# A hybrid decoder layer: start addresses of the matmul operands brought to one residue modulo 256 bytes

## The chip, the cores and the metric

The kernel runs on 1 core of a Trainium2 chip. The metric is the device time of one execution in microseconds (us). Before the change the median of 3 runs is 2601.95 us (2596.57 to 2602.49).

## What is computed

One decoder layer on 2048 tokens of width 1024, all in float32. Cut to what matters here:

```python
mod = silu(c) @ w_ada + b_ada                    # six vectors: sh_m, sc_m, gt_m, sh_f, sc_f, gt_f
h = rmsnorm(x, g_mix) * (1 + sc_m) + sh_m
q, k, v, f_logit, u = split(h @ w_in)            # 8 heads x 64; u: 32 groups x 16
log_f = log_sigmoid(f_logit + b_fgate)
attn = rmsnorm(forgetting_attention(q, k, v, log_f), g_attn_out)   # causal softmax(qk/8 + cum_i - cum_j) v
ssm = rmsnorm(s5_ssm(u, ...), g_ssm_out)         # scan, GELU z, z * sigmoid(z @ w_glu + b_glu)
x = x + gt_m * (concat(attn, ssm) @ w_out)
h = rmsnorm(x, g_ffn) * (1 + sc_f) + sh_f
gate, val = split(h @ w_up)                      # 2 x 2816
x = x + gt_f * ((silu(causal_dwconv(gate)) * val) @ w_down)
out = rmsnorm(x, g_final)
```

## The kernel before, in words

**Arithmetic.** Every large product is done in three matmuls in the fp32r format: each float32 operand is split into a rounded part (`hi`) and a remainder (`lo`), and hi·hi, hi·lo and lo·hi are summed in PSUM. Such a matmul has a stationary operand (`lhsT`, 128x128, the weights, which PE loads by a separate LDWEIGHTS) and a moving operand (`rhs`, mostly 128x512, that is 2048 bytes in each partition). The page names a matmul as out<-moving,stationary, so `up_x<-hh,w_hi` moves `hh` past weights from `w_hi`. While one matmul streams its moving operand, PE already loads the weights of the next.

**Stages.** The 2048 tokens are four blocks of 512. From 0 to about 650 us the kernel computes the modulation vectors (`ada_first`), the projections (`proj_u` with `token_rows`, L437, and `proj_qkv`, L470), the SSM's tables (`ssm_tables`) and the SSM (`ssm`), with the first attention block. From about 650 to 1820 us attention of blocks 1 to 3 (`att_max` L952; `att_main` L997, L998, a 128-wide mask matmul L1000, L1018, L1022) is woven by the scheduler between the output projection (L1232) and the feed-forward of blocks 0 and 1 (`up` L1258, `down` L1290 to L1292). From about 1960 to 2340 us `up_pair` computes the up-projection of blocks 2 and 3 together, with a two-by-two scheme of seven products (L1382, banks `up_x`, `up_y`, `up_z`). The rest is their down-projection (`down_both`, L1530 to L1532 and L1612, banks `acc_x` to `acc_z`).

**Weights.** `Weights.raw` brings a slice of the weights from HBM into one of two `w_raw` buffers of `WSLOT` = 1056 columns (L78); `split` makes `w_hi` on ScalarE (L86) and `w_lo` on VectorE (L87). All slices have at most 1024 columns but two: the weights of the columns 1536 to 1799 in `proj_u` have 4 x 264 = 1056. These go through `load` into `wu_hi` and `wu_lo` tiles of their own. A scheduler with a timeline model orders the instructions of all engines, so any edit can move others.

**Where tiles start.** Tiles lie in SBUF in pools. Pools on the left are stacked upward from a low address: `const`, `w`, `small`, `h`, the stages' own. Pools with `side="right"` are stacked downward from the top: `vq`, `att`, `late`, `ring`. A tile's start address is the sum of what lies below (or above) it, in steps of 32 bytes. A 128x512 float32 tile has 2048 bytes, so tiles of one pool keep one residue modulo 256 where all its tiles are multiples of 256 bytes, and slices of 128 columns (512 bytes) keep it too. In the built program the start addresses modulo 256 are:

| tiles of the 512-wide matmuls | pool side | before | after |
|---|---|---|---|
| `w_hi`, `w_lo` (weights) | left | 64 | 224 |
| `h_hi`, `h_lo`, `act_hi`, `act_lo`, `yt0` to `yt7`, `kx0`, 35 of 53 `ring`, 18 of 52 `hh` | left | 64 | 224 |
| `qb`, `kb`, `qa`, `ka`, `ph`, `pl`, `vv`, 28 `hh` | right | 160 | 224 |
| 18 `ring`, 4 `hh` | right | 224 | 224 |
| 2 `hh` (one in each of two longer `vq` buffers) | right | 160 and 192 | 224 and 0 |
| `w_raw` (raw weights) | left | 64 and 192 | 224 |

Modulo 512 the left tiles stand at 320 before and 480 after; the right tiles of the third row at 416 before and 224 after; the `ring` and `hh` of the fourth row at 480 both times. `wu_hi` and `wu_lo`, which are moving operands of 256 or 264 columns, start at 0 and 128 before and at 32 and 160 after, with the stationary `h_hi` and `h_lo` at 64 and 224.

Of the kernel before, what the change touches and what calls it, by code (L numbers as in the profile page):

```python
# [12 lines left out]
F32 = mybir.dt.float32  # L13
# [4 lines left out]
ALU = mybir.AluOpType  # L18
# [4 lines left out]
P = 128  # L23
# [4 lines left out]
TB = S // NB  # L28
H = 8
NG = 32  # L30
# [2 lines left out]
NFF = DFF // P  # L33
EPS = 1e-6
NEG = -1e30
WSLOT = 1056
RSQRT_MAGIC = float(0x5F3759DF)
MAGIC = 12582912.0
FFG = (6, 6, 5, 5)
# [27 lines left out]
class Weights:  # L67
# [6 lines left out]
    def raw(self, off, n, raw=None):  # L74
        if raw is None:
            raw = self.pool.tile([P, WSLOT], F32, name="w_raw", tag="w_raw", bufs=2)
        src = self.flat[off : off + P * n].rearrange("(p n) -> p n", p=P)
# [18 lines left out]
        return hi, lo  # L96

    def load(self, off, n, hi, lo):
        self.split(self.raw(off, n), n, hi, lo)

    def get(self, off, n):
        return self.split(self.raw(off, n), n)
# [18 lines left out]
def hybrid_layer(ctx, tc, x, c_t, w_ada, b_col, gains, w_flat, bf_row, a_re, a_im, log_dt,  # L121
                 sb_re, sb_im, sc_re, sc_im, dskip, glu, bglu, conv, out):
    nc = tc.nc
    V, A, G, T, Q = nc.vector, nc.scalar, nc.gpsimd, nc.tensor, nc.sync

    const = ctx.enter_context(tc.tile_pool(name="const", bufs=1))
    wpool = ctx.enter_context(tc.tile_pool(name="w", bufs=2))
    small = ctx.enter_context(tc.tile_pool(name="small", bufs=4))
    dram = ctx.enter_context(tc.tile_pool(name="scratch", bufs=1, space=DRAM))
    mark = [None]  # L130

    @contextmanager
    def behind(ins=None):
# [78 lines left out]
    off = 0  # L212
# [9 lines left out]
    for g in FFG:  # L222
        gs = []
# [5 lines left out]
    def opened(stack, name, **kw):  # L229
        return stack.enter_context(tc.tile_pool(name=name, reuse_waits="tile", **kw))  # L230
# [3 lines left out]
    vq = opened(vq_ctx, "vq", bufs=2, side="right")  # L234
# [27 lines left out]
    def max_ps():  # L262
        return am_ps()
# [3 lines left out]
    def am_ps():  # L267
        n = next(am_n) % 4 if sc_extra else 0
        if n >= 2:
            return sc_extra[n - 2]()  # L270
        return att_ps.tile([P, 512], F32, name="sc_ps", tag="sc", bufs=2)

    def vq_a(name, shape, dtype):
        return vq.tile(shape, dtype, name=name, tag="vq_a")
# [359 lines left out]
        V.tensor_tensor(out=cn, in0=cn, in1=n, op=ALU.subtract)  # L634

    r8 = const.tile([P, NPAIR], F32, name="r8")
    hb = const.tile([P, NG], F32, name="hb")

    def cmul(eng, ore, oim, ar, ai, br, bi, t):

# [7 lines left out]
    def ssm_tables(pp):  # L648
        misc_ps = prep_ps
        sh = [P, NPAIR]  # L650
        def tl(nm, shape=sh, **kw):
            return pp.tile(shape, F32, name=f"tb_{nm}", tag=f"tb_{nm}", **kw)
# [1 line left out]
        Q.dma_start(ar, a_re)  # L654
        Q.dma_start(ai, a_im)
        Q.dma_start(ld, log_dt)
        Q.dma_start(hb, bglu)
        V.tensor_scalar(out=hb, in0=hb, scalar1=0.5, scalar2=None, op0=ALU.mult)
        br, bi = tl("br", [P, NPAIR, 16]), tl("bi", [P, NPAIR, 16])
        cr, ci = tl("cr", [P, NPAIR, 16]), tl("ci", [P, NPAIR, 16])  # L660
        Q.dma_start(br, sb_re)
# [73 lines left out]
        for i0, tr_, ti_ in ((3, pl_re, pl_im), (7, ph_re, ph_im)):  # L735
            G.memset(tr_[:, :, 0:1], 1.0)
            G.memset(ti_[:, :, 0:1], 0.0)
            for i in range(4):
                m = 1 << i
# [69 lines left out]

    def ssm(sp, sps):  # L810

        fts = [sp.tile([P, 2, 2, P], F32, name=f"ft{i}", bufs=1) for i in range(2)]
        for ft in fts:
            G.memset(ft, 0.0)
# [90 lines left out]
        for p in range(NPAIR + 1):  # L905
            nxt = None
            if p < NPAIR:
                if p % 4 == 0:
                    vin = []
                    for kb in range(2):  # L910
                        t = sp.tile([P, 8, P], F32, name="vin", tag=f"vin{kb}")
                        src = u_d[kb * 1024 : (kb + 1) * 1024, (p // 4) * P : (p // 4 + 1) * P]
# [17 lines left out]
    def att_max(b, h):  # L930
# [16 lines left out]
        def part(ch, s):  # L947
            if s == 0:
                load(ch)
            n = max(256, (s + 1) * P) if ch == b else 512  # L950
            ps = max_ps()
            T.matmul(ps[:, 0:n], lhsT=qa[0:66, s * P : (s + 1) * P], rhs=ka[ch][0:66, 0:n], start=True, stop=True)  # L952
            to = mx[:, s, ch : ch + 1]
            if ch == b:
                sc = ps[:, 0 : (s + 1) * P]
                V.tensor_tensor_reduce(out=sc, in0=sc, in1=mask_q[:, (3 - s) * P :], scale=1.0, scalar=3.0 * NEG,
                                       op0=ALU.add, op1=ALU.max, accum_out=to)
            else:
                V.reduce_max(out=to, in_=ps[:, 0:n], axis=AX.X)
# [19 lines left out]
    def att_main(b, h, qa, qb, ka):  # L979
# [4 lines left out]
        def part(ch, i):  # L984
# [9 lines left out]
            cs = slice(c0, 512)  # L994
            ks = slice(i * P, (i + 1) * P)
            ps = am_ps()
            T.matmul(ps[:, cs], lhsT=kbt[:, ks], rhs=qb[:, cs], start=True, stop=False)  # L997
            T.matmul(ps[:, cs], lhsT=ka[ch][:, ks], rhs=qa[:, cs], start=False, stop=(ch != b))  # L998
# [120 lines left out]
    with tc.tile_pool(name="prep", bufs=1) as pp, tc.tile_pool(name="wu", bufs=1) as wup:  # L1119
        rows0 = load_x(2)  # L1120
        wu = load_u_weights(wup, vfu_slots[4:6])
        ada_first()
        batches = ssm_tables(pp)
        wu += load_u_weights(wup, vfu_slots[6:8])
        marks = []
        for b in (2, 3, 1):
            h = proj_u(b, rows0 if b == 2 else load_x(b), wu)
            marks.append(mark[0])
        batches(marks + marks[-1:])
        rows0 = load_x(0)  # L1130
        proj_qkv(1, h, pair_ps(qs_psum))
        ada_late(4, "gf")
        h = proj_u(0, rows0, wu)
        ada_late(3, "sf")
        forget()
        ada_cols()
        fold_gain(mod["gf"], 8)
        ada_late(2, "tm")
# [317 lines left out]
    def down_both(ap, rp, dps, misc):  # L1456
# [8 lines left out]
        def w_cols(f0, n, d):  # L1465
            raw = wpool.tile([P, WSLOT], F32, name="w_raw", tag="w_raw", bufs=2)
            o, c0 = 0, 0
            for g, m in enumerate(FFG):
                lo, hi = max(f0, c0), min(f0 + n, c0 + m)
                if lo < hi:  # L1470
                    so, sn = dn_slots[g][d]
                    view = w_flat[so : so + P * sn].rearrange("(p n) -> p n", p=P)
                    k = (hi - lo) * P
                    weights.last = Q.dma_start(raw[:, o : o + k], view[:, (lo - c0) * P : (hi - c0) * P])
                    o += k
                c0 += m
            return raw
# [231 lines left out]
    with tc.tile_pool(name="ssm", bufs=2) as sp, tc.tile_pool(name="ssm_ps", bufs=1, space=PSUM) as sps:  # L1709
        with tc.high_priority():  # L1710
            ssm(sp, sps)
# [215 lines left out]
```

## Time and profile before

| | |
|---|---|
| median of 3 runs | 2601.95 us |
| the profiled execution: time, span | 2602.08 us, 2600.4 us |
| mean granted TensorE clock of that execution | 0.98 |
| PE busy | 2506.6 us, 12107 matmuls |
| DVE busy | 2046.1 us |
| ACT busy | 1253.3 us |

A matmul's record in the trace is longer than the distance to the next one's start, since matmuls are pipelined: records overlap. Where PE never waits, the distance between starts is what a matmul costs. A row of a timeline gives start, length, engine, line, operation, out<-moving,stationary and shapes; rows of one line that follow each other with the same tiles are merged (x2). In the view of one line a row gives the shortest, median and longest record in ns. "PEclk" is the granted clock.

### The profile page before, as it was taken

How to read it: one execution, taken by the hardware profiler on the slowest of the kernel's cores; microseconds unless marked ns; L12 is line 12 of the kernel's file. 1: busy time of each engine (PE TensorE's matmuls, PEld its weight loads, DVE VectorE, ACT ScalarE, POOL GpSimd, SP SyncE). 2: the span in 40 equal slices, each digit the busy share in tenths (PEclk: the TensorE clock that was granted, in tenths of full speed). 3: DMA queues.
4: the chain of work that ended last, by engine and by line, in shares of the span. 5: the costliest groups of instructions: out<-in, count | busy, mean ns of one | idle time of the engine just before them, and what ended most of it. 6: DMA issues, size and time to landing. Idle time of an engine off the chain costs nothing.

```text
span 2600.4 us, 35785 instructions
## 1 busy us (share of the span) xinstructions
PE 2506.6 (96%) x12107; PEld 2046.8 (79%) x12107; DVE 2046.1 (79%) x3952; ACT 1253.3 (48%) x2120; POOL 152.2 (6%) x160
## 2 busy tenths in 40 slices
PE   5999899998999999999999999999989999999997
PEld 3888778887788888888878888888767888887876
DVE  7989688976787878787877777776589888886777
ACT  3423255643464545465655555556554554553213
POOL 0001000000000000000000000000002333320000
PEclk8899999998899999999999999999999999999998
DMA  8577987667456655656557555556733443448573
GB/s 300 171 240 228 287 275 212 205 195 239 165 195 219 197 191 185 196 170 217 189 192 231 183 172 191 177 177 222 242 105 126 173 155 133 158 144 294 195 272 124
DMA packets 269319, 516.36 MB, mean 199 GB/s; under 512 B 27952, under 2 KB 114864, under 8 KB 269136
## 3 DMA queue, kind: packets, MB, share of 16 engines
q1 hardware_dynamic: 267312, 508.84, 59.3%
q0 software_dynamic: 1280, 4.20, 0.4%
q8 instruction: 96, 1.57, 0.3%
q10 hardware_dynamic: 544, 1.05, 0.1%
q14 instruction: 87, 0.71, 0.1%
HBM read 374.32 MB, written 139.59 MB: 198 GB/s over the span
## 4 chain that ended last, share of the span: by engine, by line
PE 81%; DVE 8%; DMA 6%; ACT 2%; issue 2%; SPq 1%; POOL 0%; POOLq 0%; DVEq 0%; ACTq 0%
PE ff_ps L1258 18%; PE ff_ps L1232 7%; PE up_x L1382 7%; PE up_z L1382 4%; PE up_y L1382 4%; PE ff_ps L1290 3%; PE ff_ps L1292 3%; PE ff_ps L1291 3%; PE o_ps L1018 2%; PE o_ps L1022 2%; PE acc_x L1612 2%; PE vq_ps L470 2%; PE qs_ps L470 2%; DMA wada<-in_w_ada 2%; PE proj_ps L437 2%
## 5 line engine op out<-in xcount | busy, mean ns | idle before, releaser
L86 ACT CAST w_hi<-w_raw 128x1024 fp32r<-128x1024 f32 (+4 forms) x187 | 173.2, 927 | 268.6 <-DMA w_raw<-in_w_flat 69.7
L1258 PE MATMUL ff_ps<-h_hi,w_lo 128*128 128x512 f32 x704 | 277.7, 394 | 1.0 <-DMA w_lo<-wlo 1.0
L1258 PE MATMUL ff_ps<-h_hi,w_hi 128*128 128x512 f32 x704 | 277.7, 396 | 0.6 <-ACT h_hi L388 0.4
L1258 PE MATMUL ff_ps<-h_lo,w_hi 128*128 128x512 f32 x704 | 278.1, 395 | 0.0
L87 DVE TENSOR_TENSOR w_lo<-w_raw,w_hi 128x1024 fp32r<-128x1024 f32 (+4 forms) x187 | 199.7, 1068 | 62.4 <-ACT w_hi L86 51.6
L1009 DVE TENSOR_TENSOR pl<-pf,ph 128x512 fp32r<-128x512 f32 (+1 forms) x320 | 194.7, 618 | 19.8 <-ACT ph L1008 18.9
L1008 ACT CAST ph<-pf 128x512 fp32r<-128x512 f32 (+1 forms) x320 | 177.9, 568 | 61.0 <-PE o_ps L1018 57.2
L1017 DVE TENSOR_TENSOR acc<-acc,pf 128x512 f32<-128x512 f32 (+2 forms) x264 | 159.4, 605 | 44.7 <-ACT pf L1007 39.4
L1007 ACT ACTIVATE pf<-sc_ps 128x512 f32<-128x512 f32 (+3 forms) x184 | 96.3, 528 | 128.3 <-PE sc_ps L998 76.1
L1258 PEld LDWEIGHTS ff_ps<-h_hi,w_lo 128*128 128x128 f32 x704 | 133.0, 189 | 29.9 <-DMA w_lo<-wlo 1.4
L1258 PEld LDWEIGHTS ff_ps<-h_hi,w_hi 128*128 128x128 f32 x704 | 132.9, 189 | 29.4 <-DVE h_f L400 0.7
L1258 PEld LDWEIGHTS ff_ps<-h_lo,w_hi 128*128 128x128 f32 x704 | 132.9, 189 | 28.5 <-issue 0.2
L116 ACT CAST w_hi<-w_raw 128x1024 fp32r<-128x1024 f32 (+2 forms) x100 | 96.5, 965 | 110.6 <-PE ff_ps L1258 50.8
L1291 PE MATMUL ff_ps<-act_lo,w_hi 128*128 128x512 f32 x352 | 138.4, 394 | 0.0
L1292 PE MATMUL ff_ps<-act_hi,w_lo 128*128 128x512 f32 x352 | 138.4, 394 | 0.0
L1290 PE MATMUL ff_ps<-act_hi,w_hi 128*128 128x512 f32 x352 | 138.1, 395 | 0.0
L1018 PE MATMUL o_ps<-ph,vv 128*128 128x512 f32 (+1 forms) x320 | 121.0, 379 | 1.2 <-ACT ph L1008 1.2
L1022 PE MATMUL o_ps<-pl,vv 128*128 128x512 f32 (+2 forms) x312 | 117.0, 377 | 2.5 <-DVE pl L1009 2.3
L1382 PE MATMUL up_x<-hh,w_hi 128*128 128x512 f32 x352 | 112.0, 398 | 3.4 <-ACT hh L385 1.9
L1382 PE MATMUL up_z<-hh,w_hi 128*128 128x512 f32 x308 | 97.6, 398 | 2.9 <-ACT w_hi L86 2.9
L86 ACT CAST w_hi<-s 128x1024 fp32r<-128x1024 f32 (+2 forms) x66 | 62.1, 944 | 78.1 <-DVE s L1583 22.1
L437 PE MATMUL proj_ps<-wu_hi,h_hi 128*128 128x264 f32 (+1 forms) x256 | 76.2, 304 | 13.4 <-ACT h_hi L388 11.7
(673 smaller groups left out, 6863.2 us busy)
## 6 DMA issues: line engine op xcount, KB each, us to landing
w_raw<-in_w_flat SPq DMA_DIRECT2D x193, 512.0 KB
w_lo<-wlo SPq DMA_DIRECT2D x68, 512.0 KB
wlo<-w_lo SPq DMA_DIRECT2D x52, 512.0 KB
kb<-kb SPq DMA_DIRECT2D x80, 256.0 KB
vv<-v SPq DMA_DIRECT2D x80, 256.0 KB
w_raw<-in_w_flat SPq DMA_DIRECT2D x40, 384.0 KB
w_raw<-in_w_flat SPq DMA_DIRECT2D x40, 320.0 KB
wada<-in_w_ada SPq DMA_DIRECT2D x48, 256.0 KB
```

The costliest lines, as they stand in the source:

```text
L86: nc.scalar.copy(hi[:, :n], raw[:, :n])
L87: nc.vector.tensor_tensor(out=lo[:, :n], in0=raw[:, :n], in1=hi[:, :n].bitcast(F32), op=ALU.subtract)
L1008: A.copy(ph[:, cs], pf[:, cs])
L1009: V.tensor_tensor(out=pl[:, cs], in0=pf[:, cs], in1=ph[:, cs].bitcast(F32), op=ALU.subtract)
L1018: T.matmul(o_ps[:, cs], lhsT=vt[:, i, :], rhs=ph[:, cs], start=first, stop=False)
L1022: T.matmul(o_ps[:, cs], lhsT=vt[:, i, :], rhs=pl[:, cs], start=False, stop=(b > 0 and ch == b - 1 and i == 3))
L1232: mark[0] = T.matmul(ps, lhsT=lt, rhs=rt, start=(i == 0), stop=(i == 23))
L1258: T.matmul(ps, lhsT=lt, rhs=rt, start=(n == 0), stop=(n == 23))
L1290: T.matmul(ps, lhsT=a, rhs=ah[:, ts], start=(c == 0), stop=False)
L1291: T.matmul(ps, lhsT=a, rhs=al[:, ts], start=False, stop=False)
L1292: mark[0] = T.matmul(ps, lhsT=bb, rhs=ah[:, ts], start=False, stop=(c == n - 1))
L1382: mark[0] = T.matmul(ps, lhsT=lt, rhs=rt, start=(first and n == 0), stop=(n == 11), skip_group_check=not first)
```

## The change

It has four parts. `WSLOT` becomes 1024, so that a `w_raw` buffer has 4096 bytes instead of 4224; slices of 1056 columns are loaded by `load` in two halves of 528, each with a load, a cast and a subtraction of its own. Two pads are put in: 32 bytes in `const`, 192 bytes in `vq`, behind a first tile of `vq_a`'s size that fixes the order of `vq`'s parts (the third call, of 0 bytes, makes no tile). The GLU bias `hb` (128 bytes) moves from `const` to the SSM's own pool, and its load and its multiplication by 0.5 move with it from `ssm_tables` to the head of `ssm`.

```diff
-WSLOT = 1056
+WSLOT = 1024
...
     def load(self, off, n, hi, lo):
-        self.split(self.raw(off, n), n, hi, lo)
+        m = n if n <= WSLOT else n // 2
+        src = self.flat[off : off + P * n].rearrange("(p n) -> p n", p=P)
+        for c in range(0, n, m):
+            raw = self.pool.tile([P, WSLOT], F32, name="w_raw", tag="w_raw", bufs=2)
+            self.last = self.nc.sync.dma_start(raw[:, :m], src[:, c : c + m])
+            self.split(raw, m, hi[:, c : c + m], lo[:, c : c + m])
...
+    def pad(pool, n):
+        if n:
+            pool.tile([P, n // 4], F32, name="pad", tag="pad", bufs=1)
+
+    pad(const, 32)
+    pad(small, 0)
...
+    vq.tile([P, TB + 2], F32, name="gs", tag="vq_a")
+    pad(vq, 192)
...
     r8 = const.tile([P, NPAIR], F32, name="r8")
-    hb = const.tile([P, NG], F32, name="hb")
...
-        Q.dma_start(hb, bglu)
-        V.tensor_scalar(out=hb, in0=hb, scalar1=0.5, scalar2=None, op0=ALU.mult)
...
     def ssm(sp, sps):
 
+        hb = sp.tile([P, NG], F32, name="hb", bufs=1)
+        Q.dma_start(hb, bglu)
+        V.tensor_scalar(out=hb, in0=hb, scalar1=0.5, scalar2=None, op0=ALU.mult)
```

Lines of the changed kernel stand 11 to 15 further on than those of before (L1258 becomes L1273, L1382 becomes L1397).

On SP's queue in the opening, before: four loads of x, the two 1056-column slices of weights, then the stream of `w_ada`.

```order
L412 DMA xt<-in_x 128x1024 x4
L78 DMA w_raw<-in_w_flat 128x1056 x2
L293 DMA wada<-in_w_ada 128x512 x18
L654 DMA tb_ar<-in_a_re 128x16
L655 DMA tb_ai<-in_a_im 128x16
```

The same place after:

```order
L427 DMA xt<-in_x 128x1024 x4
L103 DMA w_raw<-in_w_flat 128x528 x2
L308 DMA wada<-in_w_ada 128x512 x14
L103 DMA w_raw<-in_w_flat 128x528
L308 DMA wada<-in_w_ada 128x512
L103 DMA w_raw<-in_w_flat 128x528
L308 DMA wada<-in_w_ada 128x512 x7
```

The four halves replace two whole slices; the third and the fourth half, which need a buffer that the first two have left, stand behind 14 and 15 loads of `w_ada`.

On PE in the woven stage, a place in the feed-forward of block 0 with two attention matmuls in it (`o_ps`, `qs_ps`), before:

```order
L1258 MATMUL ff_ps<-h_hi,w_hi 128x512
L1022 MATMUL o_ps<-pl,vv 128x512
L952 MATMUL qs_ps<-ka_3935,qa_3932 128x256
L1258 MATMUL ff_ps<-h_lo,w_hi 128x512
L1258 MATMUL ff_ps<-h_hi,w_lo 128x512
```

The same place after:

```order
L1273 MATMUL ff_ps<-h_hi,w_hi 128x512
L1037 MATMUL o_ps<-pl,vv 128x512
L967 MATMUL qs_ps<-ka_3943,qa_3940 128x256
L1273 MATMUL ff_ps<-h_lo,w_hi 128x512
L1273 MATMUL ff_ps<-h_hi,w_lo 128x512
```

Here nothing moves: attention's matmuls stand between the same ones of the feed-forward. Line numbers aside, about a tenth of PE's rows in the woven stage stand elsewhere, none in `up_pair` and `down_both`, and most of the rows from the SSM's tables to the first attention block, where the scheduler's order differs.

## The prediction

> **What bounds the kernel now.** The page comes first: which engine is full, and of what the chain that ended last is made.
>
> ```profile
> span 2600.4 us, 35785 instructions
> PE 2506.6 (96%) x12107; PEld 2046.8 (79%) x12107; DVE 2046.1 (79%) x3952; ACT 1253.3 (48%) x2120; POOL 152.2 (6%) x160
> PE 81%; DVE 8%; DMA 6%; ACT 2%; issue 2%; SPq 1%; POOL 0%; POOLq 0%; DVEq 0%; ACTq 0%
> ```
>
> PE is busy for 96% of the span and makes 81% of the chain. Whether it ever waits is told by the view by stretches; here one of the woven stage and one of `up_pair` (columns: length, then busy time and count of PE, PE's weight loads, DVE, ACT and POOL, then granted clock, DMA share, GB/s).
>
> ```profile
> 975.00:1040.00 65.00, 65.00 (x292) 52.65 (x291) 55.09 (x102) 37.06 (x62) 0.20 (x1) 1.00 0.57 184
> 2080.00:2145.00 65.00, 65.00 (x285) 53.20 (x284) 54.15 (x66) 33.67 (x48) 21.50 (x14) 1.00 0.42 156
> ```
>
> In both, PE is full for all 65 us at a granted clock of 1.00. So from about 650 us on only two things shorten the kernel: fewer matmuls, or less time from one matmul's start to the next. The change takes no matmul away. It only moves the places of operands, so the question is whether the distance between starts depends on them. The timeline of PE in `up_pair` answers: two runs of product `up_x`, each a repetition of two matmuls with `w_hi` and one with `w_lo`. The first has `hh` tiles at 64 modulo 256, like the weights; the second has `hh` tiles at 160 and weights at 64.
>
> ```profile
> 2040.70 0.62 PE L1382 MATMUL up_x<-hh,w_hi 128*128 128x512 f32 x2
> ...
> 2041.38 0.62 PE L1382 MATMUL up_x<-hh,w_hi 128*128 128x512 f32 x2
> ...
> 2042.06 0.62 PE L1382 MATMUL up_x<-hh,w_hi 128*128 128x512 f32 x2
> ```
>
> ```profile
> 2031.94 0.62 PE L1382 MATMUL up_x<-hh,w_hi 128*128 128x512 f32 x2
> ...
> 2032.64 0.62 PE L1382 MATMUL up_x<-hh,w_hi 128*128 128x512 f32 x2
> ...
> 2033.34 0.63 PE L1382 MATMUL up_x<-hh,w_hi 128*128 128x512 f32 x2
> ```
>
> Three matmuls take 0.68 us in the first run and 0.70 us in the second: 227 against 233 ns each, same line, same shapes, same clock, no wait. That 3% is what the change can win.
>
> The Trainium skill speaks against this: its page "TensorE: Matmul & The Clock Gate" (section "Step-by-step: what each phase is for") gives PE two independent read ports and says that "Loading the next tile's weights doesn't steal SBUF read bandwidth from the running matmul." By that rule the pair of addresses would not matter, and the time would stay; the two runs above do not agree with it.
>
> **The change part by part: the gain.** How much of the kernel pays the extra? In a run without waits a record's length is the distance to the next start plus a constant, so medians of records can be compared with that of a matched product, `up_y` (389 ns). First `up_pair`'s rows, ns as shortest/median/longest.
>
> ```profile
> L1382 PE MATMUL up_y<-hh,w_hi x176: 387/389/504, 1956.1 to 2345.1; 128*128 128x512 f32 x176
> L1382 PE MATMUL up_x<-hh,w_hi x352: 387/392/795, 1923.0 to 2350.6; 128*128 128x512 f32 x176
> L1382 PE MATMUL up_z<-hh,w_hi x308: 387/396/792, 1912.2 to 2347.9; 128*128 128x512 f32 x154
> L1382 PE MATMUL up_x<-hh,w_lo x176: 389/394/628, 1929.0 to 2350.9; 128*128 128x512 f32 x176
> L1382 PE MATMUL up_z<-hh,w_lo x154: 392/396/551, 1918.7 to 2348.1; 128*128 128x512 f32 x154
> ```
>
> Over 389: 352 x 3 + 308 x 7 + 176 x 5 + 154 x 7 ns = 5.2 us. Then the feed-forward of blocks 0 and 1, all of whose operands are at 64.
>
> ```profile
> L1258 PE MATMUL ff_ps<-h_hi,w_hi x704: 387/393/796, 694.8 to 1767.6; 128*128 128x512 f32 x176
> L1258 PE MATMUL ff_ps<-h_lo,w_hi x704: 387/393/628, 699.2 to 1767.8; 128*128 128x512 f32 x176
> L1258 PE MATMUL ff_ps<-h_hi,w_lo x704: 387/392/628, 699.6 to 1768.1; 128*128 128x512 f32 x176
> L1290 PE MATMUL ff_ps<-act_hi,w_hi x352: 387/392/504, 789.7 to 1910.6; 128*128 128x512 f32 x176
> L1291 PE MATMUL ff_ps<-act_lo,w_hi x352: 387/391/481, 789.9 to 1910.8; 128*128 128x512 f32 x176
> L1292 PE MATMUL ff_ps<-act_hi,w_lo x352: 387/391/478, 790.1 to 1911.0; 128*128 128x512 f32 x176
> ```
>
> These are matched, yet pay 704 x (4 + 4 + 3) + 352 x (3 + 2 + 2) ns = 10.2 us. The reason stands in a timeline where one attention matmul (both operands at 160) falls between the output projection's (all at 64).
>
> ```profile
> 651.28 0.39 PE L1232 MATMUL ff_ps<-act_lo,w_hi 128*128 128x512 f32 x1
> 651.50 0.39 PE L1232 MATMUL ff_ps<-yt,w_lo 128*128 128x512 f32 x1
> 651.73 0.40 PE L952 MATMUL qs_ps<-ka,qa 66*128 66x512 f32 x1
> 651.97 0.40 PE L1232 MATMUL ff_ps<-yt,w_lo 128*128 128x512 f32 x1
> 652.21 0.40 PE L1232 MATMUL ff_ps<-yt,w_hi 128*128 128x512 f32 x1
> 652.44 0.39 PE L1232 MATMUL ff_ps<-act_lo,w_hi 128*128 128x512 f32 x1
> ```
>
> Starts lie 0.22 or 0.23 us apart before it, 0.24, 0.24 and 0.23 for it and the two behind it: a change of residue is paid by the next two or three as well, matched or not. Attention's own matmuls follow.
>
> ```profile
> L1018 PE MATMUL o_ps<-ph,vv x320: 277/396/775, 345.5 to 1804.3; 128*128 128x512 f32 x128, 128*128 128x256 f32 x32
> L1022 PE MATMUL o_ps<-pl,vv x312: 277/395/774, 345.9 to 1804.7; 128*128 128x512 f32 x120, 128*128 128x256 f32 x32, 128*128 128x384 f32 x4
> L997 PE MATMUL sc_ps<-qb,kb x184: 277/396/793, 331.9 to 1782.2; 128*128 128x512 f32 x123, 128*128 128x256 f32 x41, 128*128 128x384 f32 x20
> L998 PE MATMUL sc_ps<-qa,ka x159: 277/395/628, 338.7 to 1769.8; 67*128 67x512 f32 x98, 67*128 67x256 f32 x41, 67*128 67x384 f32 x20
> ```
>
> 320 x 7 + 312 x 6 + 184 x 7 + 159 x 6 ns = 6.4 us, with the narrower ones priced too, and the same work on other banks left out; I let these cancel. Together about 22 us: the most that these rows can give. Lines I did not price (`down_both`, the output projection of blocks 2 and 3, the maxima) and the tails above the medians add an estimated 8 us, so the far end is 30.
>
> Not all of it comes. In the last row 98 of 159 attention matmuls have 512 columns; the other four in ten are narrower, and mask matmuls and transposes with operands at other residues stay as well. They will go on upsetting what follows them. I keep four tenths of the feed-forward's 10.2 us as lost (4.1 us) and nothing of the rest: 22 - 4 = 18 us from the priced rows, and 2 of the 8 unpriced. Gain: 20 us. It lies wholly on PE, in stretches where PE is full. Next late there is DVE, with 55.09 and 54.15 us of 65.00: PE would have to lose over 9 us of each 65 before DVE took over, and it loses about 0.7 (20 us over some 1900).
>
> **The other parts, at nothing, with their cover.** The split of the 1056-column slices: two more loads, casts and subtractions. In the opening:
>
> ```profile
> 4.57 1.20 SPq L78 DMA_DIRECT2D w_raw<-in_w_flat  x2
> 12.40 2.22 ACT L86 CAST wu_hi<-w_raw 128x1056 fp32r<-128x1056 f32 x2
> 34.57 0.59 PE L437 MATMUL proj_ps<-wu_hi,h_hi 128*128 128x264 f32 x1
> ```
>
> SP issues a load in 0.60 us; two more are 1.2 us of queue ahead of `w_ada` loads. The casts are done at 14.62, and PE first needs their result at 34.57: 20 us of cover for the later halves, although these now stand behind 14 `w_ada` loads. If the cover were gone, PE would wait a few us once; 0 to 3 us. As to smaller raw buffers: the loads keep their 4096 bytes a row, and I price them at nothing.
>
> The bias:
>
> ```profile
> L889 ACT ACTIVATE th<-g_ps,hb x32: 454/468/476, 385.9 to 567.5; 128x256 f32<-128x256 f32 x32
> ```
>
> Its load now stands on SP's queue just ahead of the SSM's first loads, which wait for the same thing, the pool's memory; behind it wait those and all later loads, ahead of 385.9 us. One small load more there is under 1 us. Its multiplication leaves DVE's opening for a place among evictions of k, and I price that at nothing too.
>
> The order of the first 650 us changes on every engine. That is priced by no row; it can win or lose, and I allow 5 us either way, a guess.
>
> Sum, against the profiled execution's own time of 2602.1 us (span 2600.4 and 1.7 around it; the median of the runs, 2601.95, is the same within 0.2): 2602.1 - 20 = 2582.
>
> **The rivals.** *The start itself counts, not the match* (slower). Then 64 is a good start and 224 a poor one, whatever the weights'. For it: in a run of attention matmuls matched at 160 the starts lie no closer.
>
> ```profile
> 684.42 0.40 PE L1018 MATMUL o_ps<-ph,vv 128*128 128x512 f32 x1
> 684.66 0.39 PE L997 MATMUL sc_ps<-qb,kb 128*128 128x512 f32 x1
> 684.89 0.40 PE L998 MATMUL sc_ps<-qa,ka 67*128 67x512 f32 x1
> 685.13 0.40 PE L1022 MATMUL o_ps<-pl,vv 128*128 128x512 f32 x1
> ```
>
> 0.24, 0.23 and 0.24 us. Against it: such runs are four long, follow a 256-wide matmul or a transpose, and the L1232 rows show that three matmuls at 64 pay as much after an upset. No long undisturbed run at another residue than 64 is in this trace. Price: about 6,500 matmuls (counted in the built program) have both operands at 64. The 3,168 of the feed-forward rows would go from 391 to 393 up to 396: 704 x (3 + 3 + 4) + 352 x (4 + 5 + 5) ns = 12 us; the other 3,300 from 389: 7 ns each, 23 us; less 6 for the first stage, where PE has gaps: 2602 + 29 = 2631. It decides as soon as 224 with 224 costs over 230 ns, half way.
>
> *The match counts, but over more than 256 bytes* (same). The mismatches before were of 96, 128 and 160 bytes, and these are so modulo 256 and modulo 512 alike; the trace can't tell a period of 256 from a longer one. After, left tiles stand at 480 modulo 512 and attention and most `hh` at 224, 256 apart. Then only the 18 `ring` and 4 `hh` tiles come to match, 300 matmuls of 7 ns: 2 us, 2600.
>
> *Places do nothing* (same). The two runs differ also in which end of SBUF `hh` lies; if that is what costs, only the reordering is left, 2602 give or take 5. The two ports on the page "TensorE: Matmul & The Clock Gate" of the Trainium skill (section "Step-by-step: what each phase is for") would lead to this time as well; the two `up_x` runs are what speaks against it.
>
> **How the numbers follow.** About 0.3% (8 us) is what a measurement of this kernel tells from no change. Forecast 0.72, all of it faster; longer period 0.10, end of SBUF or no effect 0.05, both same; the start itself 0.10, and a reordering that costs more than the match wins 0.03, both slower. So faster 0.72, same 0.15, slower 0.13. The range starts at 2602 - 30 - 5 = 2567 and reaches over both same cases to 2602 + 5 = 2607; outside stay the slower rival and little more.
>
> **What would show it.** Right: `up_x` and `up_z` of `up_pair` at 389 ns like `up_y`, three starts 0.68 us apart everywhere; the feed-forward's medians at 389 or 390, those of 512-wide attention matmuls at 390 to 392; PE still full from 700 to 2340 us. Wrong: `up_z` still at 396 beside 389 for `up_y` (longer period), all near 396 (the start itself), or medians at 389 with PE no longer full (another engine late).

## The result and the profile after

The changed kernel takes 2591.05 us (median of 6 runs, 2585.67 to 2594.78) beside 2602.22 us (2596.57 to 2605.57) for the kernel before in runs on the same chip: a ratio of 0.9955 with a 95% interval of 0.9938 to 0.9971. It is faster by 0.45%, 11 us, where 20 were forecast. The profiled execution took 2591.18 us.

First the head of its page and the make-up of the chain that ended last.

```profile
span 2589.5 us, 35781 instructions
PE 2494.1 (96%) x12107; PEld 2044.2 (79%) x12107; DVE 2048.6 (79%) x3954; ACT 1253.0 (48%) x2122; POOL 151.7 (6%) x160
PE 73%; DMA 10%; DVE 10%; ACT 2%; issue 2%; SPq 2%; POOL 0%; POOLq 0%; ACTq 0%; DVEq 0%
```

PE does the same 12107 matmuls in 12.5 us less busy time, and the span is 10.9 us shorter. The busy time of the weight loads and of every other engine moved by 2.6 us or less. The two stretches shown of before, in the view by stretches:

```profile
975.00:1040.00 65.00, 65.00 (x294) 53.04 (x293) 55.68 (x103) 36.60 (x62) 0.20 (x1) 1.00 0.57 189
2080.00:2145.00 65.00, 64.81 (x285) 53.19 (x284) 54.37 (x67) 33.62 (x48) 19.41 (x12) 1.00 0.45 162
```

PE is as good as full in both, at the same clock of 1.00, and in the first it starts 294 matmuls where it started 292. So a matmul has become cheaper. The view of one line shows by how much; `up_pair` first (ns as shortest/median/longest).

```profile
L1397 PE MATMUL up_y<-hh,w_hi x176: 387/389/499, 1947.7 to 2333.7; 128*128 128x512 f32 x176
L1397 PE MATMUL up_x<-hh,w_hi x352: 387/389/795, 1913.9 to 2339.2; 128*128 128x512 f32 x176
L1397 PE MATMUL up_z<-hh,w_hi x308: 387/389/792, 1903.0 to 2336.5; 128*128 128x512 f32 x154
L1397 PE MATMUL up_z<-hh,w_lo x154: 387/389/797, 1909.5 to 2336.7; 128*128 128x512 f32 x154
```

`up_x` and `up_z`, 392 and 396 before, now stand at the 389 of `up_y`. The feed-forward and attention in the woven stage:

```profile
L1273 PE MATMUL ff_ps<-h_hi,w_hi x704: 387/389/796, 696.4 to 1761.5; 128*128 128x512 f32 x176
L1305 PE MATMUL ff_ps<-act_hi,w_hi x352: 387/389/499, 789.7 to 1901.4; 128*128 128x512 f32 x176
L1033 PE MATMUL o_ps<-ph,vv x320: 274/389/775, 345.1 to 1797.7; 128*128 128x512 f32 x128, 128*128 128x256 f32 x32
L1013 PE MATMUL sc_ps<-qa,ka x159: 278/394/668, 331.8 to 1763.7; 67*128 67x512 f32 x98, 67*128 67x256 f32 x41, 67*128 67x384 f32 x20
L967 PE MATMUL sc_ps<-ka,qa x141: 277/395/797, 310.2 to 1713.5; 66*128 66x512 f32 x80, 66*128 66x256 f32 x45, 66*128 66x384 f32 x16
```

Here too the medians are 389, with two exceptions: the row whose matmuls have 67 rows stays at 394, and the maxima, with 66 rows, at 395. All their operands match like the others'.

Where the time came from, by the starts of PE's matmuls in the two traces:

| stretch, us | before | after |
|---|---|---|
| start to the first up-projection of block 0 | 694.8 | 696.4 |
| its first to its last matmul (L1258, L1273: the woven stage) | 1073.3 | 1065.5 |
| from there to the first matmul of `up_pair` | 143.2 | 140.2 |
| `up_pair`, first to last | 439.6 | 437.3 |
| from there to the end | 249.5 | 250.0 |

From 650 us on the two traces can be compared row by row. By operation, tiles and shapes PE's matmuls stand there in the same order, but for four near 1300 us; the tenth of rows that was said to stand elsewhere in the woven stage isn't in the traces. What the woven stage gained is therefore not a matter of order.

Medians hide the tails, so I also summed over all starts: for each 512-wide fp32r matmul the distance to the next start less 226.7 ns, which is the distance in long runs of matched matmuls. A matmul with a longer distance is called upset here. Distances of 287 ns and more are left out; most of them hold a wait or stand beside a narrower matmul (after the change 90, with a median of 314 ns, stand behind a mask matmul). In us:

| matmuls | before | after | distance 96 | second score, 128 rows | all 128 rows |
|---|---|---|---|---|---|
| feed-forward of blocks 0, 1 | 11.3 | 8.2 | 11.5 | 6.1 | 4.3 |
| attention (scores, `o_ps`) | 6.2 | 3.2 | 6.2 | 2.0 | 1.3 |
| attention's maxima | 1.5 | 1.3 | 1.5 | 1.2 | 0.3 |
| output projection | 2.4 | 1.0 | 2.5 | 0.8 | 0.7 |
| `up_pair` | 5.7 | 1.6 | 5.6 | 1.3 | 1.4 |
| `down_both` | 1.9 | 0.6 | 0.4 | 0.5 | 0.4 |
| first stage | 1.7 | 1.7 | 1.9 | 1.7 | 1.8 |
| sum | 30.6 | 17.5 | 29.5 | 13.5 | 10.1 |

The last three columns belong to experiments below. The change took 13.1 us off this sum; 17.5 stay, nearly half of them in the feed-forward, where every operand matches.

### The profile page after: what moved, and what is told of

Read it like the earlier page. It is cut to its first block, busy times and chain, and to the rows that moved or that the text cites. A ratio compares the mean times of both kernels' runs of the same rounds, so it can differ in the third digit from the quotient of the medians.

```text
span 2589.5 us, 35781 instructions
## 1 busy us (share of the span) xinstructions
PE 2494.1 (96%) x12107; PEld 2044.2 (79%) x12107; DVE 2048.6 (79%) x3954; ACT 1253.0 (48%) x2122; POOL 151.7 (6%) x160
## 4 chain that ended last, share of the span: by engine, by line
PE 73%; DMA 10%; DVE 10%; ACT 2%; issue 2%; SPq 2%; POOL 0%; POOLq 0%; ACTq 0%; DVEq 0%
PE ff_ps L1273 18%; PE ff_ps L1247 6%; PE up_x L1397 5%; PE up_z L1397 4%; PE up_y L1397 4%; PE ff_ps L1305 3%; PE ff_ps L1307 3%; PE ff_ps L1306 3%; PE o_ps L1033 2%; PE o_ps L1037 2%; DMA wada<-in_w_ada 2%; PE qs_ps L485 2%; PE acc_x L1627 2%; DMA w_raw<-in_w_flat 2%; PE vq_ps L485 1%
## 5 line engine op out<-in xcount | busy, mean ns | idle before, releaser
L1273 PE MATMUL ff_ps<-h_hi,w_hi 128*128 128x512 f32 x704 | 276.7, 394 | 1.0 <-ACT h_hi L403 0.8
L1273 PE MATMUL ff_ps<-h_hi,w_lo 128*128 128x512 f32 x704 | 276.7, 393 | 0.9 <-DMA w_lo<-wlo 0.9
L1273 PE MATMUL ff_ps<-h_lo,w_hi 128*128 128x512 f32 x704 | 276.8, 393 | 0.0
L1273 PEld LDWEIGHTS ff_ps<-h_hi,w_hi 128*128 128x128 f32 x704 | 132.7, 189 | 29.0 <-ACT h_hi L403 1.5
L1273 PEld LDWEIGHTS ff_ps<-h_hi,w_lo 128*128 128x128 f32 x704 | 132.8, 189 | 28.6 <-DMA w_lo<-wlo 1.3
L1273 PEld LDWEIGHTS ff_ps<-h_lo,w_hi 128*128 128x128 f32 x704 | 132.8, 189 | 27.5 <-issue 0.3
L1397 PE MATMUL up_x<-hh,w_hi 128*128 128x512 f32 x352 | 110.9, 395 | 3.4 <-ACT hh L400 1.9
L1397 PE MATMUL up_z<-hh,w_hi 128*128 128x512 f32 x308 | 96.6, 395 | 3.1 <-ACT w_hi L86 3.1
L1021 POOL MEMSET pf<- 128x128 f32 x32 | 6.6, 206 | 1401.7 <-DVE pl L1024 1171.9
```

The source lines that it names most:

```text
L1273: T.matmul(ps, lhsT=lt, rhs=rt, start=(n == 0), stop=(n == 23))
L1397: mark[0] = T.matmul(ps, lhsT=lt, rhs=rt, start=(first and n == 0), stop=(n == 11), skip_group_check=not first)
```

## The experiments

Each kernel was timed in five rounds against the kernel before on the same chip; ratios are to that, with 95% intervals. Several chips served, so kernels are compared by their ratios rather than by their medians. The edits are made in the changed kernel.

**Is it the match, and is it only the match?** Six kernels change nothing but the two pads, and keep every instruction of the changed kernel in its place. This holds for the kernel with C = 0 too, for which another order was expected: without the first pad the tiles are numbered differently, but its trace has the same rows in the same order. It is one more residue, and tells nothing of what an order is worth.

```diff
-    pad(const, 32)
+    pad(const, C)
...
-    pad(vq, 192)
+    pad(vq, V)
```

C = 128, V = 96:

> The changed kernel with pads of 128 and 96 bytes in place of 32 and 192: left and right tiles stand at 64 modulo 256, not at 224, and no instruction stands elsewhere. 18 ring and 4 hh tiles stay at 224 and so lose their match, some 300 matmuls of 7 ns, 2 us. Theory (only the match modulo 256 counts): 2591 to 2594 us, medians of the 512-wide matmuls 389 ns, up_z a little above. Rival (the start itself counts, and 224 is the good or the poor one): off by more than 5 us from the changed kernel's 2591, either way, with medians that differ from 389 in the feed-forward too.

C = 64, V = 160:

> The same with pads of 64 and 160 bytes: left and right tiles at 0 modulo 256, in the changed kernel's order. Theory (match): 2591 to 2594 us, feed-forward medians 389 ns. Rival (the start itself): if a start at a multiple of 256 is the best place, 2585 or less; if it is a poor one, over 2597.

C = 0, V = 224:

> Pads of 0 and 224 bytes: all tiles at 192 modulo 256, and, since one pad's tile is gone, another order of the scheduler's, with about 8% of PE's rows elsewhere. Theory (match): 2591 to 2594, plus or minus what an order is worth by itself, which this run bounds; I expect under 3 us. Rival (the start itself): over 5 us off.

C = 32, V = 96:

> The changed kernel with a vq pad of 96 bytes in place of 192: left tiles stay at 224, right ones go to 64, so that the distance from left to right is 96 as before the change, while the order, the split slices and the bias stay as changed. Theory (match): what the change won on 512-wide matmuls, 13.6 us summed over their starts, is lost again but for the 22 ring and hh tiles (2 us): 2602 to 2605. Rival (the gain came from the new order, the split or the smaller raw buffers): it stays at 2591.

C = 32, V = 64:

> As the one with distance 96, with a vq pad of 64 bytes: right tiles at 96, distance 128. Theory in its simple form (any mismatch costs the same 7 ns a matmul): the same 2602 to 2605. Rival (the cost grows with the distance, or half the period is harmless): more than 3 us away from the kernel with distance 96, and up_x rows with hh from the right side that lie apart from its 233 ns.

C = 32, V = 160:

> The changed kernel with a vq pad of 160 bytes: right tiles at 0, left at 224, distance 32, the smallest that can be. Theory (any mismatch modulo 256 costs alike): 2602 to 2605 us, up_x rows with hh from the right side 233 ns apart. Rival (the cost grows with the distance, or the period is shorter than 256): 2591 to 2597, 227 to 230 ns.

| left, right tiles modulo 256 | us, median | ratio to before |
|---|---|---|
| 224, 224 (the change) | 2591.05 | 0.9955 (0.9938 to 0.9971) |
| the same, timed again | 2589.95 | 0.9962 (0.9948 to 0.9975) |
| 64, 64 | 2591.85 | 0.9962 (0.9948 to 0.9976) |
| 0, 0 | 2592.99 | 0.9968 (0.9954 to 0.9981) |
| 192, 192 | 2590.53 | 0.9958 (0.9945 to 0.9972) |
| 224, 64 (distance 96) | 2600.50 | 1.0008 (0.9998 to 1.0017) |
| 224, 96 (distance 128) | 2600.80 | 1.0008 (0.9994 to 1.0022) |
| 224, 0 (distance 32) | 2600.77 | 1.0000 (0.9988 to 1.0011) |

The table has two groups and nothing between them: four residues that match, all near 0.996, and three distances that don't, all at 1.000. The start itself does not count, and in time the smallest distance costs as much as the largest; by the sum over the starts the three are not quite alike (26.6 us at 32, 29.5 at 96, 27.9 at 128). In the matching kernels at 64, 0 and 192 the 22 `ring` and `hh` tiles of the fourth row stay at 224, unmatched. The three mismatched kernels lie 1.2 to 1.5 us below the 2602 to 2605 expected; on their chips the kernel before itself took 2599.44 and 2600.26 us. Since the mismatched kernels have the changed kernel's split, bias and order, the match is the whole gain: between the groups' means, 1.0005 and 0.9961, lie 0.44%, 11 us. The other parts of the change together are worth what the kernel with distance 96 shows against before, 0.02% less to 0.17% more (0.5 us less to 4.4 more). In that kernel the 22 tiles match, and `down_both` is 1.5 us cheaper by the starts, so the other parts can be as much dearer than this.

One pair isolates which operand's place counts. With 64, 64 and with 224, 64 the `hh` tiles on the right side start at 64 alike; only the weights have moved. The same run of `up_x` in the timelines of the two, weights at 64 first, weights at 224 second:

```profile
2032.86 0.62 PE L1397 MATMUL up_x<-hh,w_hi 128*128 128x512 f32 x2
...
2033.54 0.62 PE L1397 MATMUL up_x<-hh,w_hi 128*128 128x512 f32 x2
...
2034.22 0.62 PE L1397 MATMUL up_x<-hh,w_hi 128*128 128x512 f32 x2
```

```profile
2029.86 0.62 PE L1397 MATMUL up_x<-hh,w_hi 128*128 128x512 f32 x2
...
2030.56 0.62 PE L1397 MATMUL up_x<-hh,w_hi 128*128 128x512 f32 x2
...
2031.26 0.62 PE L1397 MATMUL up_x<-hh,w_hi 128*128 128x512 f32 x2
```

Three matmuls take 0.68 us with the weights at 64 and 0.70 with the weights at 224, though the same tiles stream from the same places. Over the 492 `up_x` and `up_z` matmuls whose `hh` stands at 64 in both, the mean distance is 227.2 ns in the first kernel and 234.0 in the second. That the weights' place slows the stream is what the Trainium skill's page "TensorE: Matmul & The Clock Gate" (section "Step-by-step: what each phase is for") rules out, and the runs disagree with it.

In such runs of `up_x` a matmul's own weights and the next one's, which are loaded meanwhile, stand at the same residue. Where a run ends they part. In the three mismatched kernels there are the same 23 places in which a run of at least 13 matched matmuls at 224 (the feed-forward's, in one place the output projection's), with no wait in it, is followed by an attention matmul whose two operands stand elsewhere. The last matmul of the run matches its own weights; only those loaded while it streams stand at another residue. Its mean distance to the next start, in ns:

| distance | next weights elsewhere (23 places) | the same 23 in the changed kernel | only the next moving operand elsewhere |
|---|---|---|---|
| 32 | 234.8 | 226.7 | 226.6 (42 places) |
| 96 | 228.1 | 226.7 | 226.7 (41) |
| 128 | 232.5 | 226.7 | 226.8 (42) |

So the weights that are loaded meanwhile count. How much this one matmul pays depends on the distance, though the means over long mismatched runs are nearly alike (233.5, 234.0 and 233.1 ns over the 492 at distances 32, 96 and 128). Whether a matmul's own weights count too, these kernels can't tell.

In the woven stage of the kernel with distance 96, attention's rows and the feed-forward's are back where they were:

```profile
L1273 PE MATMUL ff_ps<-h_hi,w_hi x704: 387/393/504, 694.2 to 1767.3; 128*128 128x512 f32 x176
L1033 PE MATMUL o_ps<-ph,vv x320: 277/395/579, 345.6 to 1803.9; 128*128 128x512 f32 x128, 128*128 128x256 f32 x32
```

Each of these lines is matched in itself (224 with 224, 64 with 64), and both are slow. So a change of residue from one matmul to the next costs as well as a mismatch inside one, as the 23 places show.

**What holds the other half back?** The timeline of the changed kernel, where an attention matmul of 128 rows stands in the feed-forward:

```profile
929.51 0.39 PE L1306 MATMUL ff_ps<-act_lo,w_hi 128*128 128x512 f32 x1
929.73 0.39 PE L1307 MATMUL ff_ps<-act_hi,w_lo 128*128 128x512 f32 x1
929.96 0.39 PE L1305 MATMUL ff_ps<-act_hi,w_hi 128*128 128x512 f32 x1
930.19 0.39 PE L1037 MATMUL o_ps<-pl,vv 128*128 128x512 f32 x1
930.41 0.39 PE L1306 MATMUL ff_ps<-act_lo,w_hi 128*128 128x512 f32 x1
930.64 0.39 PE L1307 MATMUL ff_ps<-act_hi,w_lo 128*128 128x512 f32 x1
```

and where two of 66 rows do:

```profile
918.63 0.39 PE L1273 MATMUL ff_ps<-h_hi,w_lo 128*128 128x512 f32 x1
918.86 0.39 PE L1273 MATMUL ff_ps<-h_hi,w_hi 128*128 128x512 f32 x1
919.09 0.40 PE L967 MATMUL qs_ps<-ka,qa 66*128 66x512 f32 x1
919.32 0.40 PE L967 MATMUL sc_ps<-ka,qa 66*128 66x512 f32 x1
919.56 0.39 PE L1273 MATMUL ff_ps<-h_lo,w_hi 128*128 128x512 f32 x1
919.79 0.40 PE L1273 MATMUL ff_ps<-h_hi,w_lo 128*128 128x512 f32 x1
920.02 0.40 PE L1273 MATMUL ff_ps<-h_hi,w_hi 128*128 128x512 f32 x1
920.26 0.39 PE L1273 MATMUL ff_ps<-h_lo,w_hi 128*128 128x512 f32 x1
```

The first passes without a trace: 0.22 or 0.23 us from start to start throughout. In the second the four distances from 919.32 on are 0.24, 0.23, 0.23 and 0.24 us. Over the 173 stretches of matched matmuls that follow a 66-row one of 512 columns in the woven stage, the mean distances are 236, 233, 231, 228, 228, 228 ns and so on, and reach 226.7 at about the eleventh matmul; a stretch loses 20 ns in all. After the 67-row ones (146 stretches) it is the same 20 ns. After a 256-wide matmul (58) it is 16, after a mask matmul (57) 23.

The theory was therefore that matmuls of few rows upset what follows. The first test widens one of the two kinds (`eps` stands for 2.0 ** -20):

```diff
-            V.tensor_copy(rrow, pt[0:4, 0:P])
-            Q.dma_start(qa[66:67, :]...)
+            V.tensor_scalar(out=rrow, in0=pt[0:4, 0:P], scalar1=1 / eps, scalar2=None, op0=ALU.mult)
+            Q.dma_start(qa[127:P, :]...)
...
-        ts = [pool.tile([67, TB], F32R, ...)
+        ts = [pool.tile([P, TB], F32R, ...)
...
-            G.memset(t[64:67, :].bitcast(F32), 1.0)
+            G.memset(t[64:P, :].bitcast(F32), 1.0 if nm == "qa" else eps)
```

> The changed kernel with attention's second score matmul (ka, qa) over 128 rows, not 67: the tiles get 128 rows, those of qa filled with 1, those of ka with 2 to the minus 20, and the row with the maxima, scaled by 2 to the 20, goes to row 127. No matmul more or elsewhere; all scores shift by 0.00006, which the softmax drops. Theory (matmuls of fewer than 128 rows upset the matched ones behind them: 20 ns over each of 146 such stretches in the woven stage, and 6 ns on each of 203 of themselves): 4 us less than the changed kernel, 2587, and the line at 389 ns, not 395. Rival (what upsets is the switch between two stages' tiles, whatever the rows): within 1 us of the changed kernel, and the feed-forward behind it as before.

Measured: 2587.0 us, 0.9947 (0.9933 to 0.9961), as the theory had it. The interval overlaps the changed kernel's, so the trace has to carry the verdict:

```profile
L1013 PE MATMUL sc_ps<-qa,ka x159: 274/389/632, 333.6 to 1763.8; 128*128 128x512 f32 x98, 128*128 128x256 f32 x41, 128*128 128x384 f32 x20
```

394 has become 389, and the sum over the starts (table above) fell by 4.0 us, 2.1 of them in the feed-forward, none of whose matmuls was touched. The rival falls: the switch between stages is still there, the upset isn't.

The second test takes the maxima along, with one row short of full:

```diff
-            T.matmul(ps[:, 0:n], lhsT=qa[0:66, ...], rhs=ka[ch][0:66, 0:n], ...)
+            T.matmul(ps[:, 0:n], lhsT=qa[0:127, ...], rhs=ka[ch][0:127, 0:n], ...)
```

> As the one before, and the maxima's matmul (qa, ka) over 127 rows, not 66. The scheduler orders part of the woven stage anew. Theory (fewer than 128 rows upset, by how much tells the trace): if 127 rows do as little harm as 128, another 173 stretches of 20 ns and 206 times 6 ns, together 9 us less than the changed kernel, 2582; if 127 upset like 66, as the one before, 2587, with this line at 395 ns. Rival (the switch upsets): 2590 to 2592.

Measured: 2584.64 us, 0.9939 (0.9922 to 0.9956). The line shows the second case:

```profile
L967 PE MATMUL sc_ps<-ka,qa x141: 281/395/628, 310.0 to 1708.7; 127*128 127x512 f32 x80, 127*128 127x256 f32 x45, 127*128 127x384 f32 x16
```

127 rows are as bad as 66: 395 ns, and 20.8 ns lost over each of 174 stretches behind. The intervals of the two kernels overlap; the 2 us between their medians are not told apart from nothing.

The third test gives them all 128 rows, over row 127 as well:

```diff
-            T.matmul(ps[:, 0:n], lhsT=qa[0:127, ...], rhs=ka[ch][0:127, 0:n], ...)
+            T.matmul(ps[:, 0:n], lhsT=qa[:, ...], rhs=ka[ch][:, 0:n], ...)
...
             V.reduce_max(out=mneg, in_=mx[:, :, 0:nch], axis=AX.X, negate=True)
+            if id(qa) in held:
+                V.tensor_tensor(out=mneg, in0=mneg, in1=held[id(qa)], op=ALU.add)
+            held[id(qa)] = mneg
```

> As the one with 128 and 127 rows, and the maxima's matmul (qa, ka) over all 128: row 127 of qa then adds the maxima of the head two before to the scores of this one, and one small addition on VectorE for each head (30 more, 128x4) takes them off the maxima again. The scheduler orders the woven stage anew. Theory (a matmul of fewer than 128 rows upsets, 127 like 66): this line goes from 395 to 389 ns, some 215 stretches lose about 20 ns each and 205 matmuls 6 ns each, together 5 us less than the one with 127 rows, 2580. Rival (this line upsets for another reason, for it writes to other banks and follows other operands): within 1.5 us of the one with 127 rows, medians at 395.

Measured: 2591.94 us, 0.9973 (0.9962 to 0.9983). The mechanism is right and the time is a miss:

```profile
L969 PE MATMUL sc_ps<-ka,qa x141: 274/389/561, 308.9 to 1720.3; 128*128 128x512 f32 x80, 128*128 128x256 f32 x45, 128*128 128x384 f32 x16
```

395 has become 389, and the sum over the starts is 10.1 us, 7.4 below the changed kernel's. The woven stage takes 1056.5 us from the first to the last up-projection matmul, beside 1063.6 with 127 rows. But it begins at 703.7 us, not 693.8. The view by stretches says why, for 300 to 705 us and for 560 to 640, with 127 rows and then with 128:

```profile
300.00:705.00 405.00, 384.63 (x2128) 316.15 (x2127) 309.33 (x657) 197.66 (x391) 4.96 (x16) 0.97 0.71 219
560.00:640.00 80.00, 73.01 (x425) 63.68 (x424) 50.10 (x116) 33.60 (x66) 1.76 (x4) 0.91 0.75 236
```

```profile
300.00:705.00 405.00, 375.15 (x2087) 308.12 (x2086) 300.36 (x647) 192.19 (x381) 3.92 (x13) 0.97 0.71 218
560.00:640.00 80.00, 66.17 (x395) 58.43 (x394) 44.81 (x109) 31.87 (x64) 2.49 (x6) 0.87 0.71 219
```

PE is busy for 9.5 us less, and 6.8 of these lie between 560 and 640 us: there it waits. The granted clock there is 0.87 beside 0.91. PE's order in the two differs from 466 us on. Up to 550 us the full version isn't behind: the matmul of the same number starts 0.6 us earlier; at 600 us it starts 5.8 us later, at 640 us 7.8. So the last kernel kept block 0 at 127 rows, to leave that order alone:

```diff
-        nch = b + 1
+        nch, kr = b + 1, P if b else 127
...
+            T.matmul(ps[:, 0:n], lhsT=qa[0:kr, ...], rhs=ka[ch][0:kr, 0:n], ...)
```

> As the one with all 128 rows, but for blocks 1 to 3 only: block 0 keeps 127 rows and gets no addition, so that the scheduler leaves the order of the stages before the woven one as in the one with 127 rows. Theory (the 128 rows win some 5 to 7 us in the woven stage, as its span in the full version shows, and the full version lost them again before it, to an order in which the feed-forward began at 703.7 us, not 693.8): the feed-forward begins at 694 to 696, PE is in the woven stage as short as in the full version (1056 us from the first to the last up-projection matmul), and the time is 2578 to 2582. Rival (the addition and the longer wait for the maxima cost what the rows win): 2585 to 2592, with the woven stage at 1062 us or more.

Measured: 2588.41 us, 0.9954 (0.9937 to 0.9972): a miss again. The sum over the starts is 10.3 us and the woven stage takes 1059.2 us, but it begins at 700.1. The order isn't what delayed it here: PE's matmuls stand as in the kernel with 127 rows up to 688 us, and by 300 us the same matmul already starts 5.8 us later. The profiled execution is the slowest of the six (2590.89 us; the two fastest took 2583.17 and 2583.25). Nor is the start of the woven stage a firm number. In the eight traces behind the table of residues, which all have one order, it lies between 694.2 us (distance 96) and 706.2 us (distance 128, in an execution 11 us above that kernel's median).

That few rows upset is shown. That the full version lost its gain to the new order is suggested by the delay between 550 and 640 us, and not shown; which moved instruction would cost it, and where the last kernel's gain went, stays open. No version here is proven faster than the changed kernel: the two with partly widened rows have the best medians (2587.0 and 2584.6), with intervals that overlap its own.

The counter-test puts the widened second score matmul (the edit of the first test) into the kernel with distance 96:

```diff
-    pad(vq, 192)
+    pad(vq, 96)
```

> The mismatch at distance 96 (right tiles at 64, left at 224) together with attention's second score matmul over 128 rows, in the changed kernel's order. Theory (a change of residue upsets by itself, so the rows give nothing while attention and feed-forward stand at different residues): within 1.5 us of the one with distance 96 alone, 2599 to 2602. Rival (the two costs add up): 3.5 us less than that one, 2597 or less.

Measured: 2602.95 us, 1.0015 (1.0006 to 1.0024): no gain, and 1 us above the range named; the matched kernel's median fell by 3.5 (2587.0 beside 2590.53 for the kernel at 192 on the same chip), with intervals that overlap. The starts' sum falls by 1.1 us only (29.5 to 28.4). So while residues change between the stages, the rows have little left to spoil.

The changed kernel was timed again beside the last of these, with the result in the table of residues:

> The changed kernel once more, on the same chip as these: the theories agree, 2591 us, 0.996 of the kernel before. It gives the two above and the earlier ones a base of the same hour.

## Why the prediction was right in sign and too large

**The mechanism held.** Start to start in an undisturbed run depends on whether moving operand and weights start at one residue modulo 256, and the gain lies where PE is full. That the time lies in the range says little, since the range reached over two rivals' times as well. The signs named for "right" are there: `up_x` and `up_z` at 389, the feed-forward at 389, PE full. Attention's 128-row lines came to 389, better than the 390 to 392 named; those of 67 and 66 rows stayed at 394 and 395, which no part of the prediction expected.

**The terms of the sum.** `up_pair`, priced at 5.2 us, gave 4.1 by the starts, and its span is 2.3 us shorter. The unpriced lines, kept at 2 of 8, gave 2.9 (output projection 1.4, `down_both` 1.3, maxima 0.2). These were sized rightly. Too large were the two others: the feed-forward, where I counted on 6.1 of 10.2, gave 3.0, and attention, where I counted on all 6.4, gave 3.1. Together they miss by 6.4 us of the 9 that the forecast was off.

**The step that failed** is the one before the sum: "I keep four tenths of the feed-forward's 10.2 us as lost (4.1 us) and nothing of the rest". It rested on two readings. One was that a change of residue "is paid by the next two or three"; the starts show about ten. The other was to read the columns of the row with `67*128 67x512` and to count its 98 full-width matmuls among those that would be healed. It was the 67 that mattered: all 67- and 66-row matmuls went on upsetting. Behind those of 512 columns the 146 and 173 stretches in the woven stage lose 20 ns each, together 6.4 us of the 17.5 that stay. Of the feed-forward's cost 73% stayed (8.2 of 11.3), of attention's half.

**Of the 13.1 us** that the starts gave, 10.9 reached the span. 1.6 went before the woven stage, which began at 696.4 and not 694.8; the rest lies in waits that the sum leaves out.

**The parts at nothing** cost nothing that the runs can tell, by the kernel with distance 96. The split's cover was thinner than I priced it: the later halves are loaded behind the `w_ada` stream.

```profile
24.91 1.17 ACT L86 CAST wu_hi<-w_raw 128x528 fp32r<-128x528 f32 x2
32.93 0.40 PE L452 MATMUL proj_ps<-wu_hi,h_hi 128*128 128x264 f32 x1 [0.33 <-ACT h_hi L403]
```

The casts end at 26.08 and PE starts at 32.93, waiting for `h_hi`, not for weights: 7 us of cover are left of the 20. The order of the first 650 us, for which I allowed 5 us either way, cost 1.6 in the profiled execution and nothing in that of the changed kernel timed again, where the woven stage began at 694.8. That is less than traces of one order differ among themselves.

**The rivals.** "The start itself" falls with four residues that agree within 0.13%. "A longer period" falls with the change itself, whose tiles are 256 apart modulo 512 and run at 389. "Places do nothing" falls with the two groups; which end of SBUF `hh` lies in doesn't count either, since the same 492 matmuls, from the same places, changed from 234.0 to 227.2 with the weights' place alone.

## What to carry to other kernels

Where PE is full and matmuls are 512 wide, look at the distance between starts line by line: the same shape at 227 and at 233 ns can be a sign that the operands' start addresses differ modulo 256, and then pads of a few hundred bytes mend it. Count on the whole gain only in long undisturbed runs; in woven code a matmul that differs (another residue, fewer than 128 rows, narrower) costs those behind it some 16 to 23 ns in all, so count what differs in every dimension before pricing. Before you trust a small edit's gain, time one kernel that has its order without its effect, and compare orders by the rows of the traces, not by tile numbers.

## What the runs showed of the hardware

- A 512-wide fp32r matmul costs 226.7 ns from start to start in long runs in which all operands start at one residue modulo 256, whichever (0, 64, 192 and 224 alike), and 233 to 234 (means of `up_x` and `up_z` with `hh` from the right side) when moving operand and weights differ, by 32, 96 or 128 bytes alike.
- The weights that are loaded while a matmul streams count: with its own weights matched and the next ones 32, 96 or 128 bytes off, the distance to the next start was 234.8, 228.1 and 232.5 ns, and 226.7 in the same places with all matched.
- After an upset it takes some ten matched matmuls to return to 226.7, 16 to 23 ns in sum by what upset them.
- A matmul over 66, 67 or 127 rows upsets (394 or 395 ns, and 20 ns behind it); the same over 128 rows doesn't (389). The residues of all four agree. Why one row short of full does this, no run here says.
- An edit that took 7.4 us off the starts left the time where it was (2591.94 beside 2591.05 us): PE was busy for 9.5 us less from 300 to 705 us than with 127 rows. Traces of one and the same order differ by up to 12 us in when the woven stage begins (694.2 and 706.2), so a single trace can't tell where so small a loss lies.
